# Where the memory-to-memory sums of w_ff2 are issued, and which queue fetches the gates

## The chip, the core and the metric

One of the eight cores of a Trainium2 chip runs the whole kernel. Its engines work side by side, each on a program of its own: TensorE (PE; its weight loads are shown as PEld), VectorE (DVE), ScalarE (ACT), GpSimd (POOL) and SyncE (SP). Sixteen DMA engines move the data; SP and POOL only issue DMAs to them. The metric is the time of one execution in microseconds, lower is better. A run is timed on the chip several times, and one further execution is profiled.

## The reference

One layer of a decoder, 512 tokens by 1024 channels, float32. Cut to what matters:

```python
h = rms_norm(x, norm_mix)
qa, ka, va, u, qm, km, vm, gates = split_in(h @ w_in)
ya = swa_attention(qa, ka, va, sinks) @ w_o_swa              # branch A
z = gelu(s5_ssm(u, ...)) @ w_glu                             # branch B
yb = (z[..., :512] * sigmoid(z[..., 512:])) @ w_o_ssm
yc = moba_attention(qm, km, vm) @ w_o_moba                   # branch C
g = sigmoid(gates)                                           # 3 x 1024 channels
x = x + (g[..., :1024] * ya + g[..., 1024:2048] * yb + g[..., 2048:] * yc) @ w_out
h = rms_norm(x, norm_ffn)
x = x + square(relu(h @ w_ff1)) @ w_ff2                      # 1024 -> 4096 -> 1024
return rms_norm(x, norm_final)
```

## The kernel before

Matrix products run on TensorE in float32r, each as three matmuls: a weight block is split by ScalarE into a high part (`ACT.copy`) and by VectorE into what is left (a subtraction), and high x high, high x low and low x high are accumulated.

**The plan.** All that comes before the output projection is a list, `plan` (lines 223 to 242), of 81 steps, numbered from 0; `do(n, job)` (line 1027) emits one step. "u", "q", "k", "v" and "g" are 128 columns of the input projection (24 matmuls of 512 columns each); "g", b, m is block m of branch b's gates. "oa", "ob", "oc" are 128 columns of the three branch outputs (12 matmuls each), "s", "z" and "y" belong to branch B's GLU, "drain" and "start" steer the attention threads, which are woven between. The steps that matter here:

- 4 to 11: g of branch A; 18, 19, 28 to 35, 38, 39, 60, 69, 73, 76: g of branches B and C
- 20: drain of branch B's state-space part; 40 to 51: oa with y; 52 to 59: s and z
- 61 to 68: ob 0 to 7; 69: g; 70: drain; 71, 72: oc 0, 1; 73: g; 74, 75: oc 2, 3; 76: g; 77 to 80: oc 4 to 7

**Weight blocks.** The class `Stream` (line 158) fetches them on SP's queue, three blocks ahead: when the last part of a block has been split, the load of the third block after it is emitted. A load waits for a free buffer.

**Gates.** A "g" step computes tanh of half the product into `gb` (ScalarE) and, unless it is needed within four steps, stores it to DRAM from POOL's queue (line 1046, `g<-gb`, 23 of the 24). `gate_of` (line 1015) fetches it back into a tile `gl` two steps ahead of the product that it gates (line 1029), from POOL's queue. VectorE then forms (gate + 1) x product from the accumulator, which frees it (lines 1084 and 1087). There are two such accumulators, so TensorE can run one product ahead of VectorE.

**The sums of w_ff2.** The second feed-forward product uses a scheme of the Strassen kind on quarters of 512 x 512 of `w_ff2`, which wants sums of quarters. They are formed in DRAM, in tiles `td[q]`, q = 0 to 6, with four places each, by DMAs alone: a copy of a quarter, or an accumulating DMA that adds one (line 1153) or another place of `td` (lines 1156, 1159). These are POOL's. `w2_sums` (line 1144) is a generator of 56 DMAs of 512 KB, 28 copies and 28 that add; a `next` emits one. From step 14 on, one is emitted after each step (line 1170), so the last belongs to step 69. The first reader of `td` is `load_q` (line 1471), in the second feed-forward product; `load_t` (line 1506) reads the other places later still.

**Order.** The schedule is by hand (`tc.manual_schedule()`): each engine runs its instructions in the order in which they are emitted, and waits at an instruction for what that one needs. SP's and POOL's DMAs are issued in that order too; a DMA that waits holds back all that follow on its queue.

**Behind the plan.** The output projection (lines 1311 to 1334) is four row blocks t of 8 k-steps, 48 matmuls each; its weights `wor` and the residual `x` are fetched on SP's queue from the end of steps 71, 74 and 75 on. Within it the first blocks of `w_ff1` are fetched and split (`parts.ahead`, line 1327). The first feed-forward product runs over `steps`: 16 whole ones (two for each of 8 column blocks), 77 of a Strassen-like scheme over pairs of blocks (7 each), and 4 whole ones. Four of them are written out, the loop at line 1523 runs over the rest, 93.

Of the kernel before, what the change touches and what calls it, by code (L numbers as in the profile page):

```python
# [19 lines left out]
def trunk(ctx: ExitStack, tc: tile.TileContext, x, norm_mix, w_in, sinks, lam_re, lam_im,  # L20
# [50 lines left out]
    class Engine:  # L71
# [42 lines left out]
    PE, ACT, DVE, POOL, SP = (Engine(e, n) for e, n in (  # L114
        (nc.tensor, "PE"), (nc.scalar, "ACT"), (nc.vector, "DVE"), (nc.gpsimd, "POOL"),
        (nc.sync, "SP")))
# [13 lines left out]
    def B8(shape, name, dt=F32):  # L130
        return slot("B8", 18, big.tile(shape, dt, tag="B8", name=nm_(name), bufs=18))

    def B4(shape, name, dt=F32):
        return slot("B4", 11, big.tile(shape, dt, tag="B4", name=nm_(name), bufs=11))

    def B2(shape, name, dt=F32):
        return slot("B2", 7, big.tile(shape, dt, tag="B2", name=nm_(name), bufs=7))
# [4 lines left out]
    def PS(tag, name, shape=(128, 512)):  # L142
        b = {"acc": 2, "S": 3, "T": 2, "O": 1}[tag]
        return slot(tag, b, psum.tile(list(shape), F32, tag=tag, name=nm_(name), bufs=b))
# [13 lines left out]
    class Stream:  # L158
# [7 lines left out]
        def add(self, w, k, cols, width):  # L166
            nk = k // 128
            for c0 in cols:
                if c0 % width == 0 or not self.jobs or self.jobs[-1][1] is not w:
                    self.blocks.append((w, nk, c0, width))  # L170
                for k0 in range(0, nk, 4):
                    self.jobs.append((len(self.blocks) - 1, w, k0, c0))
# [50 lines left out]
    plan = [("u", m) for m in range(4)]  # L223
# [29 lines left out]
    for job in plan:  # L253
        if job[0] in where:
            w, k, c, width = where[job[0]]
# [84 lines left out]
    def stt(o, a, s, b, op0, op1):  # L340
        DVE.scalar_tensor_tensor(o, a, s, b, op0=op0, op1=op1)
# [13 lines left out]
    MUL, ADD, SUB = ALU.mult, ALU.add, ALU.subtract  # L355
# [645 lines left out]
    gd = {(b, m): dram.tile([128, 512], F32, name=f"g{b}_{m}") for b in range(3) for m in range(8)}  # L1001
    gsb, ga, fin, sg = {}, [], {}, {}
# [12 lines left out]
    def gate_of(b, m):  # L1015
        if (b, m) not in gsb:
            gsb[b, m] = B2([128, 512], "gl")
            POOL.dma_start(gsb[b, m], gd[b, m])
        return gsb[b, m]

    def prep_y(m):
# [71 lines left out]
    def more():  # L1093
        if all(x_.over for x_ in build) and not threads["ssm"]:
            threads["ssm"] = [weave(ssm_run(g)) for g in ((0, 2), (1, 3))]
# [38 lines left out]

    NQ, FROM, EACH = 7, 14, 1
    td = [dram.tile([128, 2, 4, 512], F32, name=f"td{q}") for q in range(NQ)]

    def w2_of(q, h, c):  # L1140
        return w_ff2[0][512 * q:512 * q + 512, 512 * c:512 * c + 512].rearrange(
            "(s h p) c -> h p s c", h=2, p=128)[h]

    def w2_sums():
        for r in range(NQ + 3):
            if r < NQ:
                for h, js in ((0, (0, 1)), (1, (2, 3))):
                    for c in range(2):
                        POOL.dma_start(td[r][:, :, js[c]], w2_of(r, h, c))
                        yield  # L1150
            if 0 <= r - 1 < NQ:
                for j, h in ((0, 0), (1, 1)):
                    POOL.dma_start(td[r - 1][:, :, j], w2_of(r - 1, h, 1), accum_op=ADD)
                    yield
            if 0 <= r - 2 < NQ:
                POOL.dma_start(td[r - 2][:, :, 3], td[r - 2][:, :, 0], accum_op=ADD)
                yield
            if 0 <= r - 3 < NQ:
                POOL.dma_start(td[r - 3][:, :, 2], td[r - 3][:, :, 3], accum_op=ADD)
                yield  # L1160

    sums2 = w2_sums()

    ut = B8([128, 4, 4, 128], "ut")
    u_t[0] = ut
    build = [weave(ssm_b()), weave(ssm_c()), weave(ssm_phasors())]
    for n, job in enumerate(plan):
        do(n, job)
        more()
        if n >= FROM:  # L1170
            for _ in range(EACH):
                next(sums2, None)
    for _ in sums2:
        pass

    class Parts:

# [85 lines left out]
    steps, late = [], []  # L1263
# [15 lines left out]
    def tail_part(t, acc, ns):  # L1279
        xs = x2[t // 2][:, t % 2, :]  # L1280
        s_, c_ = st[:, t:t + 1], st[:, 4 + t:5 + t]
        if 0 in ns:
            xn_[t] = B4([128, 1024], "xn")
        for n in ns:
            sl = slice(n * 512, n * 512 + 512)
            stt(xs[:, sl], acc[n], 0.5, xs[:, sl], MUL, ADD)
            ACT.activation(xn_[t][:, sl], xs[:, sl], AF.Square, accum_out=s_)
            if n == 0:
                stt(c_, s_, 1.0 / 1024, eps, MUL, ADD)
# [21 lines left out]
    for t in range(4):  # L1311
        acc = [PS("acc" if t % 2 else "S", "xo") for _ in range(2)]
        for ns in (((0, 1),) if t < 3 else ((0,), (1,))):
            for k in range(8):
                if t == 0 and 2 <= k < 6:
                    prep_w(k + 2)
                a_h = mx_t["h", k // 4][:, k % 4, t * 128:t * 128 + 128]
                a_l = mx_t["l", k // 4][:, k % 4, t * 128:t * 128 + 128]
                b_h, b_l = wo_t["h", k // 2][:, k % 2, :], wo_t["l", k // 2][:, k % 2, :]
                for s_, w_, f in ((a_h, b_h, 0), (a_h, b_l, 1), (a_l, b_h, 2)):  # L1320
                    for n in ns:
                        PE.matmul(acc[n], s_, w_[:, n * 512:n * 512 + 512],
                                  start=(k == 0 and f == 0), stop=(k == 7 and f == 2))
                if k == 5 and t > 0 and 0 in ns:
                    turn(t - 1, prev)
                if 0 in ns and (t, k) in AHEAD:
                    parts.ahead(1)
            tail_part(t, acc, ns)
        if t == 0:
            for _ in range(3):  # L1330
                parts.load()
            h2h = [B8([128, 4, 512], "h2h", F32R) for _ in range(2)]
            h2l = [B8([128, 4, 512], "h2l", F32R) for _ in range(2)]
        prev = tail(t)
# [143 lines left out]
    def b_prep(i, h):  # L1478
        if i < NP:
            t = wb[i, h] = B8([128, 2, 1024], "w2s", F32R)  # L1480
            src = wq[i][:, 2 * h:2 * h + 2].rearrange("p c n -> p (c n)")
            split(t[:, 0], t[:, 1], src)
# [37 lines left out]
            load_t(n + 3)  # L1520

    xs_ = x_sums()
    for u, p in steps[4:]:
        if len(u) == 2:
            for _ in xs_:
                pass
        f1_step(u, p)
        if len(u) == 1:
            next(xs_, None)
        if (u, p) == late[-1]:  # L1530
            load_q(0)
            load_q(1)
            a_sums(0)
            b_prep(0, 0)
        if (u, p) == ((30,), 1):
            a_prep(0)
    while later:
        later.pop()()
    b_prep(0, 1)
    load_q(2)  # L1540
    gf = B4([128, 1024], "gf")
# [22 lines left out]
    for i in range(NP):  # L1564
        q, s_ = divmod(i, 2)
# [30 lines left out]
    for n in range(3 * NQ):  # L1596
        j, q = divmod(n, NQ)
# [72 lines left out]
```

## Time and profile before

| | us |
|---|---|
| median of 3 runs | 825.02 |
| lowest and highest | 822.97, 827.93 |
| the profiled execution | 822.13 |
| its span, from the first to the last instruction | 820.4 |

| engine | busy us | share of the span |
|---|---|---|
| TensorE | 776.0 | 95% |
| VectorE | 590.2 | 72% |
| ScalarE | 439.5 | 54% |
| POOL | 105.1 | 13% |

The profile names an instruction by its engine, its line (L110 is the helper that emits all compute instructions, L90 the one that emits DMAs) and its tiles, out<-in. `x12` is a count; `[1.65 <-DVE gl L110]` says that the engine was idle for 1.65 us before the instruction, and what ended that. PEclk is the granted share of TensorE's full clock. In the table of DMA queues q0 is POOL's queue and q1 SP's. A busy TensorE is not one at its full rate, since matmuls are pipelined and wait within the pipe as well.

### The profile page before, as it was taken

How to read it: one execution, taken by the hardware profiler on the slowest of the kernel's cores; microseconds unless marked ns; L12 is line 12 of the kernel's file. 1: busy time of each engine (PE TensorE's matmuls, PEld its weight loads, DVE VectorE, ACT ScalarE, POOL GpSimd, SP SyncE). 2: the span in 40 equal slices, each digit the busy share in tenths (PEclk: the TensorE clock that was granted, in tenths of full speed). 3: DMA queues.
4: the chain of work that ended last, by engine and by line, in shares of the span. 5: the costliest groups of instructions: out<-in, count | busy, mean ns of one | idle time of the engine just before them, and what ended most of it. 6: DMA issues, size and time to landing. Idle time of an engine off the chain costs nothing.

```text
span 820.4 us, 11497 instructions
## 1 busy us (share of the span) xinstructions
PE 776.0 (95%) x4210; PEld 662.0 (81%) x4210; DVE 590.2 (72%) x1176; ACT 439.5 (54%) x848; POOL 105.1 (13%) x163
## 2 busy tenths in 40 slices
PE   5999999999899999996799999999999999999996
PEld 5887777878788887785678888899999978888885
DVE  6985697774785688773358445788788688976775
ACT  7496633373665566650134434556565565665633
POOL 5131010170021345032210000000000000000000
PEclk9999999999999999999999999999999999999998
DMA  9452371479366999979995004133333476645702
GB/s 248 120 150 74 118 193 56 138 155 249 99 150 183 228 289 246 270 180 207 259 340 185 5 22 127 40 101 103 96 105 102 155 256 205 206 146 187 257 1 103
DMA packets 116249, 130.29 MB, mean 159 GB/s; under 512 B 5304, under 2 KB 87264, under 8 KB 116192
## 3 DMA queue, kind: packets, MB, share of 16 engines
q1 hardware_dynamic: 99232, 85.22, 34.1%
q0 software_dynamic: 16768, 44.06, 22.8%
q8 instruction: 33, 0.54, 0.3%
q10 hardware_dynamic: 192, 0.27, 0.1%
q14 instruction: 24, 0.20, 0.1%
HBM read 119.30 MB, written 37.49 MB: 191 GB/s over the span
## 4 chain that ended last, share of the span: by engine, by line
PE 68%; DVE 14%; DMA 9%; ACT 5%; issue 3%; POOL 1%; DVEq 0%; ACTq 0%; POOLq 0%
PE f L110 36%; PE acc L110 18%; PE xo L110 5%; DVE w L110 4%; DMA wraw<-in_w_in_dram 3%; DMA td<-in_w_ff_dram 2%; DVE own L110 2%; DMA f1raw<-in_w_ff_dram 2%; PE s L110 2%; DVE p L110 2%; PE po L110 2%; PE pt L110 1%; PE y L110 1%; DMA gl<-g 1%; DVE t L110 1%
## 5 line engine op out<-in xcount | busy, mean ns | idle before, releaser
L110 PE MATMUL acc<-hh,w 128*128 128x512 f32 (+1 forms) x672 | 217.7, 390 | 9.7 <-DVE k L110 4.5
L110 PEld LDWEIGHTS acc<-hh,w 128*128 128x128 f32 x672 | 125.8, 191 | 34.9 <-issue 6.8
L110 PE MATMUL acc<-hl,w 128*128 128x512 f32 (+1 forms) x336 | 129.4, 385 | 2.1 <-DVE hl L110 2.1
L110 PE MATMUL f<-h2h,f1w 128*128 128x256 f32 (+1 forms) x456 | 102.9, 313 | 2.8 <-DVE vz L110 2.6
L110 DVE TENSOR_TENSOR w<-wraw,w 128x512 fp32r<-128x512 f32 x112 | 74.8, 686 | 18.6 <-ACT w L110 18.2
L110 ACT CAST w<-wraw 128x512 fp32r<-128x512 f32 x112 | 67.2, 618 | 35.6 <-DMA wraw<-in_w_in_dram 21.9
L110 PEld LDWEIGHTS f<-h2h,f1w 128*128 128x128 f32 x456 | 76.8, 191 | 8.6 <-ACT f1w L110 3.1
L110 PE MATMUL f<-w2s,s 128*128 128x512 f32 x336 | 79.2, 390 | 0.7 <-DVE w2s L110 0.6
L110 PEld LDWEIGHTS f<-w2s,s 128*128 128x128 f32 x336 | 62.9, 188 | 14.6 <-DVE w2s L110 1.0
L110 PEld LDWEIGHTS acc<-hl,w 128*128 128x128 f32 x336 | 64.2, 191 | 12.8 <-DVE hl L110 2.5
L110 PE MATMUL f<-h2l,f1w 128*128 128x256 f32 (+1 forms) x228 | 71.4, 313 | 0.3 <-DVE h2l L110 0.3
L110 PE MATMUL f<-xt,f1w 128*128 128x256 f32 x528 | 67.1, 283 | 0.0
L110 PEld LDWEIGHTS f<-xt,f1w 128*128 128x128 f32 x528 | 65.1, 192 | 0.1
L110 PE MATMUL acc<-o,w 128*128 128x512 f32 x192 | 48.2, 396 | 0.1
L110 ACT ACTIVATE act<-act 128x512 f32<-128x512 f32 (+1 forms) x54 | 31.8, 589 | 27.8 <-DVE act L110 26.8
L110 PEld LDWEIGHTS f<-h2l,f1w 128*128 128x128 f32 x228 | 43.5, 191 | 3.0 <-DVE h2l L110 0.5
L110 ACT CAST w2s<-wq 128x1024 fp32r<-128x1024 f32 x28 | 28.8, 1050 | 27.2 <-PE f L110 12.7
L110 PE MATMUL f<-w2s,av 128*128 128x512 f32 x168 | 42.7, 389 | 0.0
L110 PEld LDWEIGHTS acc<-o,w 128*128 128x128 f32 x192 | 35.1, 188 | 7.9 <-issue 0.9
L110 DVE TENSOR_TENSOR f1w<-f1raw,f1w 128x512 fp32r<-128x512 f32 x53 | 36.0, 685 | 7.4 <-ACT f1w L110 7.4
L90 POOL DMA_DIRECT2D g<-gb x23 | 12.8, 557 | 217.2 <-ACT gb L110 180.6
L110 DVE TENSOR_TENSOR w2s<-wq,w2s 128x1024 fp32r<-128x1024 f32 x28 | 33.5, 1220 | 8.9 <-ACT w2s L110 8.9
(222 smaller groups left out, 1469.1 us busy)
## 6 DMA issues: line engine op xcount, KB each, us to landing
td<-in_w_ff_dram POOLq DMA_DIRECT2D x42, 512.0 KB, 9.9
wraw<-in_w_in_dram SPq DMA_DIRECT2D x40, 512.0 KB, 4.5
f1raw<-in_w_ff_dram SPq DMA_DIRECT2D x32, 512.0 KB, 4.2
tq<-td SPq DMA_DIRECT2D x21, 512.0 KB, 4.5
td<-td POOLq DMA_DIRECT2D x14, 512.0 KB, 12.5
wq<-in_w_ff_dram SPq DMA_DIRECT2D x14, 512.0 KB, 4.4
g<-gb POOLq DMA_DIRECT2D x23, 256.0 KB, 3.5
gl<-g POOLq DMA_DIRECT2D x23, 256.0 KB, 9.9
```

The costliest lines, as they stand in the source:

```text
L90: return f(o, *a, **k)
L110: return f(o, *a, **k)
```

## The change

Three things. Gate loads are issued by SP in place of POOL. The sums are emitted at other places: after steps 13 to 17, after every second step from 26 to 80, once in each of the four row blocks of the output projection, and before every fifth of the 93 steps of the loop over the first feed-forward product; what is left would follow that loop. And their order within the generator is another one: the sums that `load_q` reads first, all seven q, then those of place 1, which is read late. The 56 DMAs are the same.

```diff
     def gate_of(b, m):
         if (b, m) not in gsb:
             gsb[b, m] = B2([128, 512], "gl")
-            POOL.dma_start(gsb[b, m], gd[b, m])
+            SP.dma_start(gsb[b, m], gd[b, m])
         return gsb[b, m]
...
-    NQ, FROM, EACH = 7, 14, 1
+    NQ = 7
+    SUMS_AT = set(range(13, 18)) | set(range(26, len(plan), 2))
...
     def w2_sums():
-        for r in range(NQ + 3):
-            if r < NQ:
-                for h, js in ((0, (0, 1)), (1, (2, 3))):
-                    for c in range(2):
-                        POOL.dma_start(td[r][:, :, js[c]], w2_of(r, h, c))
-                        yield
-            if 0 <= r - 1 < NQ:
-                for j, h in ((0, 0), (1, 1)):
-                    POOL.dma_start(td[r - 1][:, :, j], w2_of(r - 1, h, 1), accum_op=ADD)
-                    yield
-            if 0 <= r - 2 < NQ:
-                POOL.dma_start(td[r - 2][:, :, 3], td[r - 2][:, :, 0], accum_op=ADD)
-                yield
-            if 0 <= r - 3 < NQ:
-                POOL.dma_start(td[r - 3][:, :, 2], td[r - 3][:, :, 3], accum_op=ADD)
-                yield
+
+        def copy(q, j, h, c):
+            POOL.dma_start(td[q][:, :, j], w2_of(q, h, c))
+
+        def add(q, j, src):
+            POOL.dma_start(td[q][:, :, j], src, accum_op=ADD)
+
+        for q in range(NQ + 1):
+            if q < NQ:
+                copy(q, 0, 0, 0)
+                yield
+                copy(q, 3, 1, 1)
+                yield
+                add(q, 0, w2_of(q, 0, 1))
+                yield
+                copy(q, 2, 1, 0)
+                yield
+            if q:
+                add(q - 1, 2, td[q - 1][:, :, 3])
+                yield
+            if q < NQ:
+                add(q, 3, td[q][:, :, 0])
+                yield
+        for q in range(NQ + 1):
+            if q < NQ:
+                copy(q, 1, 0, 1)
+                yield
+            if q:
+                add(q - 1, 1, w2_of(q - 1, 1, 1))
+                yield
...
     for n, job in enumerate(plan):
         do(n, job)
         more()
-        if n >= FROM:
-            for _ in range(EACH):
-                next(sums2, None)
-    for _ in sums2:
-        pass
+        if n in SUMS_AT:
+            next(sums2, None)
...
                 if 0 in ns and (t, k) in AHEAD:
                     parts.ahead(1)
+                if 0 in ns and k == 3:
+                    next(sums2, None)
...
-    for u, p in steps[4:]:
+    for n, (u, p) in enumerate(steps[4:]):
+        if n % 5 == 0:
+            next(sums2, None)
...
     while later:
         later.pop()()
+    for _ in sums2:
+        pass
     b_prep(0, 1)
```

## Rows read from the trace of the kernel before

**Rows 1.** The page: the span, and POOL's DMA queue (packets, MB, share).

```profile
span 820.4 us, 11497 instructions
...
q0 software_dynamic: 16768, 44.06, 22.8%
```

**Rows 2.** Busy time by stage: stretch, length, engines with instructions, PEclk, DMA share, GB/s.

```profile
361.00:438.00 77.00, 65.88 (x269) 51.68 (x267) 39.57 (x61) 19.98 (x34) 18.68 (x26) 0.96 0.99 265
438.00:485.00 47.00, 46.71 (x218) 38.50 (x217) 25.17 (x40) 18.74 (x36) 0.00 (x0) 1.00 0.14 37
485.00:640.00 155.00, 151.86 (x1130) 145.27 (x1129) 118.37 (x203) 91.91 (x176) 0.00 (x0) 1.00 0.34 94
```

**Rows 3.** Waits, 361 to 438 us: total, times, longest.

```profile
PE acc L110 <- DVE gl L110: 11.0, 5, 4.4
...
DVE gl L110 <- DMA gl<-g: 27.3, 7, 7.0
```

**Rows 4.** Timeline of TensorE, 361 to 440 us: start, length, instruction, idle before.

```profile
388.26 4.58 PE L110 MATMUL acc<-z,w 128*128 128x512 f32 x12 [2.88 <-DVE gl L110]
...
408.53 0.50 PE L110 MATMUL acc<-hh,w 128*128 128x512 f32 x1 [4.40 <-DVE gl L110]
...
427.12 11.04 PE L110 MATMUL acc<-o,w 128*128 128x512 f32 x48
```

**Rows 5.** Timeline of POOL, 363 to 405 us.

```profile
365.64 1.52 POOL L90 DMA_DIRECT2D gl<-g  x1
...
396.89 0.88 POOL L90 DMA_DIRECT2D td<-td  x1 [8.93 <-DMA td<-td]
397.45 0.91 POOL L90 DMA_DIRECT2D gl<-g  x1
```

**Rows 6.** Timeline of SP, then of POOL, 320 to 352 us.

```profile
326.42 19.21 SPq L90 DMA_DIRECT2D wraw<-in_w_o_ssm_dram  x4
...
348.86 0.57 POOL L90 DMA_DIRECT2D gl<-g  x1 [19.10 <-PE po L110]
```

**Rows 7.** TensorE's waits, 140 to 146 us, then 200 to 212 us.

```profile
PE acc L110 <- DVE k L110: 1.9, 1, 1.9
...
PE acc L110 <- DVE k L110: 2.5, 1, 2.5
```

**Rows 8.** Timeline of POOL: three of the gate stores.

```profile
288.69 0.55 POOL L90 DMA_DIRECT2D g<-gb  x1 [5.80 <-ACT gb L110]
...
363.36 0.56 POOL L90 DMA_DIRECT2D g<-gb  x1 [11.62 <-ACT gb L110]
...
419.06 0.55 POOL L90 DMA_DIRECT2D g<-gb  x1 [12.19 <-ACT gb L110]
```

**Rows 9.** DMA, 380 to 400 us: queues; issues with size and median landing.

```profile
q0 software_dynamic: 1552, 3.37, 83.9%
q1 hardware_dynamic: 1770, 1.15, 23.7%
...
wraw<-in_w_in_dram SPq DMA_DIRECT2D x1, 512.0 KB, 19.2
```

**Rows 10.** DMA, 405 to 440 us, then 485 to 640 us.

```profile
f1raw<-in_w_ff_dram SPq DMA_DIRECT2D x4, 512.0 KB, 9.5
...
q1 hardware_dynamic: 28180, 14.36, 33.2%
```

**Rows 11.** Timeline of SP from 420 us, then of ScalarE from 455 us.

```profile
428.13 68.00 SPq L90 DMA_DIRECT2D f1raw<-in_w_ff_dram  x7
...
458.64 0.63 ACT L110 CAST f1w<-f1raw 128x512 fp32r<-128x512 f32 x1
...
463.94 1.13 ACT L110 CAST f1w<-f1raw 128x512 fp32r<-128x512 f32 x2
```

## The prediction

> **What bounds the kernel now.** I read the page first, then busy time by stage, then TensorE's waits, then the DMA queues. The page gives a span of 820.4 us [rows 1]; the whole profiled execution took 822.13 us. TensorE works nearly all the time, so a gain can only come from a stretch in which it starves. By stage, 361 to 438 us (the gate products "ob" and "oc" of branches B and C, and the last three gate projections) has 65.88 us of TensorE work in 77.00 us, at a mean granted clock of 0.96, with the DMA engines 0.99 busy; the output projection behind it has 46.71 of 47.00 us and DMA at 0.14; the first feed-forward product has 151.86 of 155.00 us and DMA at 0.34 [rows 2]. So one stage starves, it is the one whose DMA engines are full, and the two stages behind it have DMA time to spare.
>
> What starves it: TensorE waits five times, 11.0 us, for VectorE's step that reads a gate tile and frees the accumulator, and VectorE waits 27.3 us, seven times, for gate loads [rows 3]. Why the gate loads are late: they stand in POOL's queue between the sums. A load issued at 365.64 us is behind the sums of the steps before it. The sum at 396.89 us first had POOL sit 8.93 us for another sum to land, and the gate load right behind it, at 397.45 us, is the one for which TensorE stood still until 408.53 us [rows 4, 5]. The chip adds a second charge: after the longer idle times the granted clock was at the lower of its two levels, 1.2 instead of 2.4 GHz. Twelve matmuls from 388.26 us took 4.58 us, against 11.04 us for 48, or 2.76 us for 12, later in the stage [rows 4].
>
> **The change, part by part.**
>
> Gate loads. 23 loads leave POOL's queue for SyncE's; no load is added, each step has the loads it had. On POOL they no longer stand behind a wait for a landed sum. The bound of the gain is the 11.0 us of waits plus the clock: 0.04 of 77 us is 3.1 us [rows 2, 3]; 14.1 us together. I do not take all of it. Five sums still go out behind the gate store of 363.36 us (steps 60 to 68), where ten stood before, and the gate loads still need DMA time beside them; one stall of the smaller kind (11.0 / 5 = 2.2 us) may be left. I take 12.5 us, ends 8 and 14.1.
>
> What is queued behind them on SyncE: the weight blocks, `w_out` and `x`. On POOL a gate load's wait for a free buffer (released by the attention product) lasted 19.10 us once, but POOL was early there: what counts is how late the buffer comes free against the weight load behind it. That wait ended at 348.86 us; SyncE's fourth `w_o_ssm` load had gone out by 345.63 us, so at worst 3.2 us of hold [rows 6]. The buffers of the later gate loads are released by the gate products four to five steps before, so nothing waits long. I cost this at nothing, since weight blocks are fetched three blocks ahead; if that cover were gone it would be about 3.2 us, once.
>
> Sums taken out of the early part. In place of one sum a step from step 14 on, there are five at steps 13 to 17 and one every second step from 26. So behind the branch-B drain one sum follows where eight did. There a weight block landed late and the wait of TensorE for the K projection was 2.5 us, against 1.9 us for the same step of branch A with idle DMA engines [rows 7]. The gain is 0.6 us, and at most another 1.7 us if the clock no longer drops afterwards; I take 1 us, ends 0 and 2.3.
>
> Where the sums go. This is the part to be careful with. The text says "every fifth feed-forward step", but a DMA on POOL waits for nothing that TensorE does: it is held only by what stands ahead of it in POOL's program and by the sum whose result it needs. What paced POOL were the gate stores, which wait for ScalarE, as at 288.69, 363.36 and 419.06 us [rows 8]; the one at 419.06 us (step 73) is the last store. In the changed kernel POOL has only sums after it. Counting the generator: 5 in steps 13 to 17, 28 in steps 26 to 80, 4 in the output projection, 19 in the feed-forward steps, 56 as before; 29 of them are issued up to step 72, and 27 stand behind the last store. These 27 will run as one train, starting near 419 - 13 = 406 us, not spread to 640 us.
>
> Its length: POOL's queue moved 44.06 MB in 22.8% of 820.4 us, 4.25 us a MB, so a sum of 0.524 MB takes 2.2 us of all 16 engines [rows 1]. 27 of them are 60 us at the least. Some of that time goes to SyncE's loads and some to waiting for a landed sum (an accumulate waits for the copy it adds to); I expect the train to end between 480 and 500 us. Before, nothing of POOL's moved in that time.
>
> What the train meets: two `w_out` loads, `x`, the last gate loads, then the first `w_ff1` blocks. With sums in flight the queues take turns packet by packet: from 380 to 400 us 1552 packets of POOL's and 1770 of SyncE's went through, taking 83.9% and 23.7% of the engines, 0.173 and 0.043 us a packet [rows 9]. A `w_ff1` block is fetched in packets of 14.36 MB / 28180 = 510 bytes, 1028 of them [rows 10]: alone 1028 x 0.043 / 16 = 2.8 us of the queue, with a sum's packet before each one 1028 x 0.216 / 16 = 13.9 us. So the first three blocks land about 11, 22 and 33 us later than they do now. Now they are issued from 428.13 us on, land 9.5 us later (median), and ScalarE casts the first at 458.64 us and needs the second within the pair at 463.94 us [rows 10, 11]: 21 us of cover for the first, about 24 us for the second. The first is just covered. The second, and the third behind it, may come some us late, and with ScalarE standing the residual sums behind it stand as well. I price this at 3 us, plus 2 us for the second pair of `w_out` loads and the last gate loads, which now follow `x` in SyncE's queue: 5 us, ends 0 and 18 (the second end is the rival's below).
>
> The Trainium skill, "DMA: Bandwidth & Descriptors", section "Queues, rings and completion order", says that each DMA engine goes round its queue rows one packet at a time. The packet counts above agree with it, 1552 against 1770 [rows 9]. By that rule the gate loads lose something by the move: on POOL's row they had a turn of their own beside the weights, on SyncE's they share one turn with the weights. It speaks for the second rival below, whose time is worked out there from rows.
>
> The sum: 12.5 + 1 - 5 = 8.5 us off the profiled execution's 822.13 us, 813.6 us. The median of the runs before is 825.02 us, 2.9 us above the profiled one, so 816.5 us stands beside it.
>
> **The rivals.**
>
> First: the train is harmless. For it speaks that the output projection now leaves the engines 0.86 idle and that the first `w_ff1` block has 21 us of cover [rows 2, 11]. Then 14.1 + 1.5 us are gained, 809.5 us.
>
> Second, on the other side: the train and SyncE's order starve the end of the stage. The gate loads of the last "oc" steps stand behind two `w_out` loads and four `x` loads in one queue. 4 MB in 4 KB packets are 1024 packets; with a sum's packet each, 1024 x 0.173 / 16 = 11.1 us are added. Behind them the third and the fourth `w_out` load (another 5.5 us) and the `w_ff1` blocks wait, whose second one then comes 22 + 16 - 24 = 14 us after it is needed. If the 11.1 us fall on TensorE in full, and half of the 14 us, the cost is 18 us: 13.5 - 18 = 4.5 us slower, 829.5 us. It decides from the point where the gate load of "oc" 5 lands later than two gate products (5.5 us) after its turn. Against it: now, too, these loads share the engines with gate loads and a sum from 405 to 440 us, and TensorE doesn't wait after 409 us.
>
> Third: the gate loads are as late on SyncE as on POOL, behind weight blocks, of which one took 19.2 us from issue to landing among the sums [rows 9]. Then the 11 us stay and only the clock and the early part change; with the train's 5 us it is no change, 825 us. Against it: only five sums, not ten, meet this stage.
>
> **How the numbers follow.** A measurement of this kernel can tell about 0.5%, 4.1 us, from no change. Forecast (4 to 13 us gained) 0.44; harmless train 0.18; no change 0.17; slower 0.21. Faster holds the first two, 0.62. The likeliest time is 816.5 us, its own range 812 to 821. The range of all cases: below, the full bounds with a harmless train, 825.02 - 14.1 - 2.3 = 808.6, less the 2 us by which the fastest run before lies under the median, 806.6; above, the slower rival, 829.5 us, cut to 829 so that under 2 in 10 is left out.
>
> **What the profile of the changed kernel would show.** TensorE's waits for the gate step gone or under 3 us from 361 to 425 us, granted clock back at 0.98 or more there; POOL's queue busy without a gap from about 406 to 490 us and empty after it, not one sum every fifth step to 640 us; `w_ff1` blocks landing in 12 us or more up to 490 us, and ScalarE waiting for one or two of them. I am wrong if the gate step is still waited for, if sums really come one by one up to 640 us, or if TensorE stands for more than 8 us between 425 and 500 us.

## The result and the profile after

The changed kernel takes 804.27 us (median of four runs, 800.91 to 807.01) against 825.67 us (822.97 to 827.93) of the kernel before: ratio 0.974, 95% interval 0.9692 to 0.9789. The forecast was 816.5 us and the range 806.6 to 829.0. The direction was right, the size was not: 21 us came instead of 8.5, and the time lies below the range. The profiled execution took 800.91 us, 21.2 us less than the one of before.

The page of the changed kernel: the span, POOL's busy tenths in 40 slices, SyncE's queue (q1), POOL's queue (q0), and the group of POOL's sums with their idle time.

```profile
span 799.1 us, 11512 instructions
...
POOL 6041020040011231001212131000000000000000
...
q1 hardware_dynamic: 102544, 91.26, 37.1%
q0 software_dynamic: 14928, 38.03, 20.8%
...
L90 POOL DMA_DIRECT2D td<-in_w_ff_dram x42 | 36.3, 1078 | 76.2 <-DMA td<-in_w_ff_dram 75.5
```

Busy time by stage, columns as in [rows 2]; the last row is the stretch that holds the same TensorE work as the first of [rows 2].

```profile
361.00:438.00 77.00, 77.00 (x345) 63.88 (x344) 49.57 (x72) 26.88 (x42) 14.43 (x18) 1.00 1.04 307
438.00:485.00 47.00, 46.14 (x258) 39.71 (x257) 22.89 (x39) 17.92 (x38) 12.05 (x14) 1.00 0.89 192
485.00:640.00 155.00, 151.56 (x1101) 143.81 (x1100) 120.47 (x206) 94.95 (x176) 2.09 (x2) 1.00 0.46 127
356.00:416.50 60.50, 60.50 (x269) 50.10 (x268) 39.55 (x61) 20.20 (x34) 11.98 (x15) 1.00 1.03 320
```

The waits of the changed kernel, 361 to 438 us, the longest three and VectorE's for the gate tile's product.

```profile
POOL td L90 <- DMA td<-in_w_ff_dram: 31.5, 3, 11.0
POOL g L90 <- ACT gb L110: 19.3, 2, 10.9
ACT mh L110 <- DVE ga L110: 17.5, 8, 3.1
DVE gl L110 <- PE acc L110: 15.8, 10, 4.9
```

POOL's timeline around its last gate store and at its end.

```profile
395.83 0.59 POOL L90 DMA_DIRECT2D g<-gb  x1 [8.40 <-ACT gb L110]
396.41 1.44 POOL L90 DMA_DIRECT2D td<-in_w_ff_dram  x2
407.83 1.77 POOL L90 DMA_DIRECT2D td<-in_w_ff_dram  x2 [9.99 <-DMA td<-in_w_ff_dram]
408.97 1.61 POOL L90 DMA_DIRECT2D td<-td  x1
418.35 0.90 POOL L90 DMA_DIRECT2D td<-td  x1 [7.77 <-issue]
...
493.95 1.05 POOL L90 DMA_DIRECT2D td<-in_w_ff_dram  x1 [5.45 <-DMA td<-in_w_ff_dram]
```

The stage that starved [rows 2, 3] starves no more. VectorE now waits for TensorE's product where it waited for the gate load, TensorE waits for neither, and the granted clock is 1.00. TensorE's 269 matmuls of that stretch take 60.50 us; before they took 77.00 us, 65.88 of them busy. So 16.5 us came from there: 11.1 us of idle time and 65.88 - 60.50 = 5.4 us by which the matmuls themselves took longer before. The lower clock is only a part of these: a mean of 0.96 over 77 us lacks 0.04 x 77 = 3.1 us (3.5 at most, by the rounding), and the clock can't have cost more than that. Another part is the new start after each wait. Before, two groups of twelve matmuls ran behind waits of 1.2 and 1.7 us at a granted clock of 1.00 and took 3.00 us each, against 2.76 us for twelve in an unbroken run [rows 4]. Five such starts are about 1.2 us; some 1 us stays unexplained. The first of the two groups, and the mean clock around it:

```profile
374.35 3.00 PE L110 MATMUL acc<-z,w 128*128 128x512 f32 x12 [1.65 <-DVE gl L110]
...
360.00:380.00 20.00, 17.18 (x75) 13.58 (x75) 10.48 (x17) 6.18 (x12) 10.11 (x13) 1.00 0.86 160
```

The rest is read from the starts of the same matmul in both traces: 1.0 us lost in the first 60 us, 1.6 won between 165 and 175 us, 3.6 won between 187 and 260 us, 0.8 won up to 361 us, 16.5 won up to 438 us, and from there to the end nothing above 0.8 us either way. The train of sums ran from 396.41 to 493.95 us and then nothing; it cost TensorE no more than these 0.8 us. The sums that read `w_ff2` itself stood 76.2 us in all before they went out, 75.5 of them for a copy that had to land; a group like that is not among the large ones of the kernel before.

One effect of the change stands neither in its text nor in the prediction. The kernel weaves the attention threads into the plan by a model of time of its own (`account`, `step`), which counts every DMA that is emitted. With one sum behind the drain of branch B in place of eight, 219 of TensorE's 4210 matmuls stand in another order, between 197 and 257 us. The kernels below with eight sums there have the order of before, the others that of the changed kernel. It matters little: with the new order of the sums, the kernels with eight sums there win 4.1 to 4.2 us between 187 and 260 us, the changed kernel 3.6.

### The profile page after: what moved, and what is told of

It is laid out like the page before. It is cut to its first block, busy times and chain, and to the rows that moved or that the text cites. A ratio compares the mean times of both kernels' runs of the same rounds, so it can differ in the third digit from the quotient of the medians.

```text
span 799.1 us, 11512 instructions
## 1 busy us (share of the span) xinstructions
PE 768.6 (96%) x4210; PEld 658.5 (82%) x4210; DVE 589.3 (74%) x1176; ACT 440.0 (55%) x848; POOL 92.2 (12%) x140
## 4 chain that ended last, share of the span: by engine, by line
PE 77%; DVE 13%; DMA 4%; ACT 3%; issue 2%; DVEq 0%; ACTq 0%
PE f L110 37%; PE acc L110 26%; PE xo L110 5%; DVE w L110 4%; DVE own L110 2%; DMA f1raw<-in_w_ff_dram 2%; PE s L110 2%; PE po L110 2%; PE pt L110 2%; DMA wraw<-in_w_in_dram 2%; PE y L110 1%; DVE t L110 1%; PE pg L110 1%; DVE pr L110 1%; DVE p L110 1%
## 5 line engine op out<-in xcount | busy, mean ns | idle before, releaser
L110 PE MATMUL acc<-hh,w 128*128 128x512 f32 (+1 forms) x672 | 215.3, 386 | 3.2 <-DVE k L110 1.9
L90 POOL DMA_DIRECT2D td<-in_w_ff_dram x42 | 36.3, 1078 | 76.2 <-DMA td<-in_w_ff_dram 75.5
```

The source lines that it names most:

```text
L90: return f(o, *a, **k)
L110: return f(o, *a, **k)
```

## The experiments

A sum below is one of the 56 memory-to-memory copies or accumulates of `w_ff2`. The change has three parts: the queue of the gate loads (POOL or SyncE), the places of the sums (one a step, or thinned out and a train), and the order of the sums among themselves. The prediction priced the first two. The ratio stands for each kernel against the runs of before on the same chip. The last three columns are what the profiled execution wins (or loses, with a minus) against the profiled one of before in three stretches of before's time, read from the starts of the same matmuls.

| order of the sums | gate loads on | places | us | ratio, 95% interval | 300 to 335 | 361 to 438 | 438 to 485 |
|---|---|---|---|---|---|---|---|
| old | POOL | old (before) | 825.67 | 1 | | | |
| old | SyncE | old | 827.37 | 0.9998 (0.9956 to 1.004) | -7.2 | 5.3 | 0.0 |
| old | SyncE | new | 823.71 | 0.9996 (0.9962 to 1.0031) | -3.1 | 15.9 | -17.3 |
| new | POOL | old | 815.91 | 0.9914 (0.9882 to 0.9946) | -3.0 | 6.4 | 0.1 |
| new | SyncE | old | 809.97 | 0.9804 (0.9746 to 0.9863) | 0.0 | 7.2 | 0.0 |
| new | POOL | new | 809.10 | 0.9786 (0.9745 to 0.9828) | 0.0 | 10.2 | -0.3 |
| new | SyncE | new (after) | 804.27 | 0.974 (0.9692 to 0.9789) | 0.0 | 16.5 | 0.0 |

The eighth combination (old order, POOL, new places) was not run. The stretches show what the ratios hide. In the starved stage (361 to 438 us) queue and places do nearly all, 15.9 of 16.5 us with the old order; queue and order with a sum a step win 7.2 us. What the new order adds to queue and places lies elsewhere: 17.3 us in the output projection and 3.1 us near 320 us are no longer lost.

### The queue alone, and the sums alone

Gate loads on SyncE, nothing else:

```
-            POOL.dma_start(gsb[b, m], gd[b, m])
+            SP.dma_start(gsb[b, m], gd[b, m])
```

> The gate loads alone go from POOL's queue to SyncE's; the sums stay one a step from step 14 on. Theory (two separate gains, both needed: gate loads off POOL, and fewer sums beside the two stages; and a train of sums behind the last gate store that costs nothing): the waits of TensorE for the gate step from 361 to 438 us shrink from 11.0 us but don't vanish, because ten sums, not five, still take turns with the loads there; the K projection's wait at 204 us stays at 2.5 us. 815 to 820 us. Rival A (the move of the gate loads is all that counts): gate waits zero, clock 1.00 in that stage, 16.5 us gained, 806 to 810 us. Rival B (the gate loads are late on either queue while ten sums run beside them; only the new places of the sums count): 823 to 826 us.

Measured: 827.37 us, ratio 0.9998. The theory's 815 to 820 us were missed; rival B's 823 to 826 us are the nearest. The move that my forecast, together with thinner sums, put at 12.5 us brings nothing by itself. Its TensorE waits, 300 to 345 us and then 361 to 438 us:

```profile
PE acc L110 <- DVE ga L110: 3.5, 1, 3.5
...
PE acc L110 <- DVE gl L110: 7.1, 3, 6.8
```

From 361 to 438 us the same matmuls lose 5.3 us less than before, so something is won there; but 7.2 us are lost between 300 and 335 us, 3.5 of them in a wait that before did not have. DMA issues from 303 to 309 us, with the median landing:

```profile
gl<-g SPq DMA_DIRECT2D x2, 256.0 KB, 15.4
td<-in_w_ff_dram POOLq DMA_DIRECT2D x1, 512.0 KB, 24.9
```

A gate load is off POOL's queue and still takes 15.4 us. No wait of POOL's is in front of it any more, but weight blocks share its queue, and in these 6 us 379 packets of POOL's queue went beside 367 of SyncE's.

The changed kernel with the gate loads back on POOL (the same line, the other way):

> The sums stand where the change puts them; the gate loads stay on POOL's queue. Theory (two separate gains): the early gain of about 5 us up to 236 us is there in full; from 361 to 438 us gate loads still stand behind accumulates that wait for a landed copy, now every second step, so 5 to 10 us of the 16.5 us come: 806 to 814 us. Rival A (the move of the gate loads is all that counts in the stage): gate waits stay near 11 us, 818 to 821 us. Rival B (only the sums count): gate waits gone, 802 to 806 us.

Measured: 809.1 us, 0.9786, as the theory had it. Of the stage's 16.5 us, 10.2 came without the move of the gate loads. Rival A, that only the move counts, is out. So is rival B, that only the sums count: TensorE still waits 3.3 us for gate products, and 5 us more come with the move. I had still not seen the third part.

### The order of the sums

The changed kernel's order with the old places (one sum a step from step 14), gate loads on SyncE:

```
-    SUMS_AT = set(range(13, 18)) | set(range(26, len(plan), 2))
+    SUMS_AT = set(range(14, len(plan)))
```

> The gate loads on SyncE's queue, and the changed kernel's order of the sums (which copy comes before which accumulate), but one sum a step from step 14 on, as before. Only the order differs from the first experiment, which was 827.4 us. Theory (with no gate load on POOL nothing but gate stores and landed sums holds the sums back, eight of them are in flight at once, and the gate tiles on SyncE's queue take 15 us and more): the new waits near 320 us and near 395 us come back, together over 8 us: 815 to 828 us. Rival (the order's own waits are what thins the sums): no such wait, 801 to 810 us.

Measured: 809.97 us, 17 us below the first experiment, which differs in the order alone; my theory missed it and the rival was right in time. In the trace it was right near 320 us, where the wait is gone. In the stage TensorE still waits for gate products (361 to 438 us):

```profile
PE acc L110 <- DVE gl L110: 7.0, 3, 5.3
```

The timeline of POOL from 292 to 330 us, first the kernel with the old order, a few rows:

```profile
310.78 0.91 POOL L90 DMA_DIRECT2D td<-td  x1 [3.42 <-DMA td<-td]
316.36 0.89 POOL L90 DMA_DIRECT2D td<-td  x1 [4.68 <-DMA td<-td]
318.07 0.72 POOL L90 DMA_DIRECT2D td<-in_w_ff_dram  x1 [0.82 <-DMA td<-in_w_ff_dram]
321.55 0.69 POOL L90 DMA_DIRECT2D td<-in_w_ff_dram  x1 [2.76 <-DMA td<-in_w_ff_dram]
```

and then the one with the new order:

```profile
294.69 1.77 POOL L90 DMA_DIRECT2D td<-in_w_ff_dram  x2
305.23 1.78 POOL L90 DMA_DIRECT2D td<-in_w_ff_dram  x2 [8.78 <-DMA td<-in_w_ff_dram]
306.38 1.60 POOL L90 DMA_DIRECT2D td<-td  x1
314.25 0.89 POOL L90 DMA_DIRECT2D td<-td  x1 [6.28 <-DMA td<-in_w_ff_dram]
```

Both wait for landed sums, but not for the same ones. In the old order an accumulate of this stretch stands nine or more sums behind the one that it needs. By the numbers POOL stops only when about eight are in flight (24.9 us to landing, with one issued every 2.9 us from 293 to 325 us: 24.9 / 2.9 = 8.6). One goes out whenever one lands, so the queue should hardly ever be empty. In the new order an accumulate stands two to five sums behind the one that it needs, so POOL issues three and then stops 6 to 11 us until one of these has landed.

The other two corners. The new order alone, all else as before:

> The kernel before with the changed kernel's order among the sums and nothing else: gate loads on POOL's queue, one sum a step. Theory (the new order's waits hold the sums, but on POOL's queue the gate loads stand behind just these waits): the K projection's wait at 204 us goes (4 us), the gate waits from 361 to 438 us stay or grow, 815 to 824 us. Rival (the order is the whole gain): 803 to 810 us.

Measured: 815.91 us, 0.9914, within the theory's numbers. The wait at 204 us is gone. TensorE's waits for gate products shrank from 11.0 to 6.8 us, where the theory had them stay or grow. That what is left comes from gate loads standing behind the new waits fits, but no run isolates it.

The changed kernel with the old order:

```
-            if q < NQ:
-                copy(q, 0, 0, 0)
-                yield
...
+            if r < NQ:
+                for h, js in ((0, (0, 1)), (1, (2, 3))):
+                    for c in range(2):
+                        POOL.dma_start(td[r][:, :, js[c]], w2_of(r, h, c))
+                        yield
...
```

> The changed kernel (gate loads on SyncE's queue, the sums at the changed places) with the order of before among the sums: four copies of a block of rows first, their accumulates one to three rounds later. Theory (the new order is a third part of the change, with a gain of its own: an accumulate soon behind its copy makes POOL wait for a landed sum, so that few sums are in flight, while in the old order eight are in flight and SyncE's loads take 20 us and more): gate tiles and weight blocks land later again, TensorE waits for them, and the train packs closer: 808 to 818 us. Rival (the places and the queue suffice, the order only mattered with a sum in each step): 800 to 806 us, without gate waits.

Measured: 823.71 us, 0.9996: without the order the other two parts together bring nothing, which is beyond both expectations. The stage is cured here too; TensorE's wait for gate products, 361 to 438 us:

```profile
PE acc L110 <- DVE gl L110: 0.3, 1, 0.3
```

But 3.1 us are lost near 320 us, and the train takes the rest back in the output projection. The waits from 438 to 485 us of this kernel's own time:

```profile
ACT f1w L110 <- DMA f1raw<-in_w_ff_dram: 27.8, 3, 12.2
...
PE h L110 <- DVE xn L110: 10.9, 1, 10.9
```

The matmuls that ran from 438 to 485 us before run from 420 to 485 us here and lose 17.3 us. This is one half of my second rival: ScalarE stands at a `w_ff1` cast, and the residual sums stand behind it. The other half, 11.1 of its 18 us, was to come from late gate loads, and those are not late (0.3 us); it had about 7 us for the `w_ff1` blocks. That 18 and 17.3 lie so close is luck.

The DMA queues and the `w_ff1` loads from 430 to 480 us, in this kernel:

```profile
q0 software_dynamic: 3555, 8.45, 86.3%
q1 hardware_dynamic: 3579, 1.96, 19.5%
...
f1raw<-in_w_ff_dram SPq DMA_DIRECT2D x3, 512.0 KB, 49.8
```

in the changed kernel:

```profile
q0 software_dynamic: 2800, 6.91, 69.0%
q1 hardware_dynamic: 5325, 2.68, 21.0%
...
f1raw<-in_w_ff_dram SPq DMA_DIRECT2D x5, 512.0 KB, 12.9
```

Where POOL's queue always holds a sum, each packet of SyncE's has one of POOL's before it, 3555 to 3579. A packet of POOL's is 0.863 x 50 x 16 / 3555 = 0.194 us, one of SyncE's 0.044 us, so a block of 1028 packets takes 1028 x 0.238 / 16 = 15.3 us; three in the queue are 46 us, and they took 49.8. Where POOL's queue runs empty, SyncE sends nearly two packets for one.

Do fewer sums run in the changed kernel, then? Not over the whole train. POOL's queue in the changed kernel, 396 to 494 us, then in the one with the old order, 399 to 495 us:

```profile
q0 software_dynamic: 5617, 14.15, 64.9%
...
q0 software_dynamic: 5826, 13.32, 71.0%
```

The bytes are nearly the same; how they are spread is not. By the DMA packets of the traces, from 430 to 480 us the kernel with the old order has no moment without a packet of POOL's, the changed kernel 5.6 us.

The Trainium skill, "DMA: Bandwidth & Descriptors", section "Queues, rings and completion order", says that an engine goes round the queue rows for which it has work. The prediction took the first half of that sentence; these rows agree with the second half too: with a row that is empty for a part of the time, its neighbour sent 5325 packets to 2800, not 3579 to 3555.

### By what the order acts

To the changed kernel with the old order, I added a copy of 512 bytes after every third sum, from a sum's result to a scratch tensor, so that POOL has to wait as in the new order. First it reads the first of the three, then the third:

```
+            done.append((q, jj))
+            if len(done) % 3 == 0:
+                q_, j_ = done[-3]          # then: done[-1]
+                POOL.dma_start(brk[...], td[q_][0:1, 0, j_, 0:128])
```

(The text calls the changed kernel with the old order the eighth experiment.)

> The kernel of the eighth experiment (changed queue, changed places, order of before among the sums; 823.7 us), and in addition POOL copies 512 bytes of the first of every three sums to a scratch tensor, so that it has to wait for that sum to land before it goes on. The added copies are work that the reference doesn't need. Theory (the order matters through these waits alone: they empty POOL's queue from time to time, and SyncE's loads then go without a sum's packet before each of theirs): sums land in 7 to 14 us, the w_ff1 blocks in 15 to 27 us instead of 41 to 56 us, TensorE no longer stands 17 us at 438 to 485 us: 801 to 809 us. Rival (something else in the order, such as which rows are copied next to which): 815 to 825 us.

Measured: 816.39 us, 0.991: within the rival's range, above the theory's. Two sums are still in flight at each wait, POOL's packets hold 77.4% of the engines' time from 430 to 480 us, and `w_ff1` blocks take 27.1 us. The output projection loses 3.0 us in place of 17.3, but 7.6 us are lost behind it, up to 560 us. So this run does not decide.

> As the last experiment, but the added copy of 512 bytes reads the third of every three sums, not the first, so that POOL waits until its queue is empty (it is work that the reference doesn't need). With the first of three, two sums were still in flight at each wait, and half of the difference came: 816.4 us between 823.7 (old order) and 804.3 us (new order). Theory (what counts is how often POOL's queue runs empty): the w_ff1 blocks land in 10 to 27 us, no stand of TensorE at 415 to 540 us beyond 3 us, 802 to 809 us. Rival (the waits give half at most, the rest is something else in the order): 812 to 818 us again.

Measured: 811.53 us, 0.9845 (0.9768 to 0.9922), four runs from 808.56 to 818.59: between the two ranges, half a microsecond below the rival's. The time decides nothing, but the trace of the profiled execution (810.16 us) is the theory's up to 515 us. The same view of the queues, 430 to 480 us:

```profile
q0 software_dynamic: 2425, 6.38, 56.1%
q1 hardware_dynamic: 5554, 2.80, 20.3%
...
f1raw<-in_w_ff_dram SPq DMA_DIRECT2D x5, 512.0 KB, 8.5
```

From 187 to 515 us every matmul starts 3.0 us after the same one of the changed kernel: nothing is won or lost there. (Nearly all of the 3.0 us are two falls of the clock, near 146 and 173 us.) What it has more, 6.6 us between 515 and 549 us, goes with the train's length: with these waits its last sum goes out at 532 us, not at 494 us, and TensorE waits 7.7 us for VectorE's `vz` from 485 to 640 us, the wait of the longer trains below. So in this execution the waits by which POOL's queue runs empty account for all that the order does up to there; the order's own waits do it in less time.

### How long a train is free

The changed kernel with no sum in the steps of the plan, all 56 in the train; and with 16 ahead and 40 in the train:

```
-    SUMS_AT = set(range(13, 18)) | set(range(26, len(plan), 2))
+    SUMS_AT = set(range(13, 18)) | set(range(26, 48, 2))     # 40; for 56: none in the plan
...
+    for _ in range(17):                                      # 27 for 56
+        next(sums2, None)
```

> The changed kernel, but no sum runs in the planned steps: all 56 stand behind the last gate store in POOL's queue, so the train is twice as long. Theory (the train of 27 was free only because the loads of the w_ff1 blocks have about 20 us of cover, and one landed 0.02 us ahead of its use): a train of 56 sums runs from about 400 to beyond 590 us, each w_ff1 block takes near 14 us instead of 9.5 us while two are needed every 10.4 us, the cover runs out, TensorE waits in the first feed-forward product: 820 to 850 us. Rival (sums beside that product cost nothing at any length): 800 to 805 us, with the loads late by no more than in the changed kernel.

Measured: 849.02 us, ratio 1.026.

> The changed kernel with 40 sums behind the last gate store instead of 27: the ones of plan steps 48 to 80 are taken out of the plan and stand right behind it. Theory (the loads of the w_ff1 blocks have a cover that the train of 27 just uses up: one landed 0.02 us ahead of its use; 56 in the train cost 45 us): the train ends near 545 us, blocks issued from 500 to 540 us take 12 to 15 us instead of 4 to 9, TensorE waits in the first feed-forward product for 10 to 25 us: 812 to 828 us. Rival (the train of 27 is far from its limit; that of 56 costs so much because it reaches some later stage): 800 to 806 us.

Measured: 819.09 us, 0.9899. Both as the theory had it. The longest wait of TensorE from 485 to 640 us, first with 56 sums in the train, then with 40:

```profile
PE f L110 <- DVE vz L110: 38.2, 6, 11.0
```

```profile
PE f L110 <- DVE vz L110: 14.5, 5, 10.2
```

A train of 27 is nearly free, 13 more cost 15 us, 16 further ones 30 us. The limit is near 27: in the changed kernel ScalarE waits once for a `w_ff1` block, at the train's end.

```profile
487.12 0.62 ACT L110 CAST f1w<-f1raw 128x512 fp32r<-128x512 f32 x1 [2.79 <-DMA f1raw<-in_w_ff_dram]
```

### The early part

The changed kernel with eight sums behind the drain of branch B again, where the prediction saw the gain of its second term, and seven fewer in the train:

```
-    SUMS_AT = set(range(13, 18)) | set(range(26, len(plan), 2))
+    SUMS_AT = set(range(13, 18)) | set(range(20, 28)) | set(range(28, len(plan), 2))
```

> The changed kernel, with one sum behind each of steps 20 to 27 again (eight behind the drain of branch B, where the change leaves one or two); so seven sums fewer are in the later train. Theory (the eight sums made the K projection's weight block land late, and the 3.4 us lost at 204 us, K wait and the lower clock after it, come from that): the wait of 2.5 us and the lower clock return at 200 to 210 us, 3.5 to 5.5 us slower than the changed kernel, 808 to 810 us. Rival (the K wait is not of the sums, and the early gain is another chance of the clock): no wait at 204 us, 803 to 805 us.

Measured: 801.64 us, 0.9706 (0.9672 to 0.9739), below the rival's range too. The theory fell: with the new order the eight sums bring no wait of the K projection back. Beside the changed kernel on one chip:

> The changed kernel once more, to stand beside the next run on the same chip: 801 to 806 us. If the fall of the clock at 170 us is chance, it may or may not be there; all else as in the first execution.

> The changed kernel with eight sums behind the drain of branch B (the third experiment again), beside the changed kernel on the same chip. Theory (in the new order seven more sums at 177 to 206 us cost nothing there, and seven fewer in the train take away the small waits at 540 to 580 us, 0.7 us): within 2 us of the changed kernel, more likely below it. Rival (they bring the K projection's wait back in some executions): 3 us above it.

Measured: 802.77 us (802.25 to 803.92) and 800.94 us (799.48 to 801.99). Beside each other this version is some 2 us below the changed kernel, six runs each without an overlap. That is less than it looks: of the 2.6 us between the two profiled executions, 1.6 are the clock at 170 us, which fell in the changed kernel's and not in the other's (below), and over all runs of the two kernels the ranges overlap (800.91 to 807.01 us and 799.09 to 805.03 us in the first ones). The two profiled executions in which the clock stayed up, 800.91 and 799.64 us, differ by 1.3 us. That this version is faster is likely, and not shown.

The kernel before once more:

> The kernel before, unchanged, one more execution with a profile. The profiled execution of before had the lower clock for part of 170 to 187 us, and then a K projection's wait of 2.5 us with the lower clock again at 204 us; every variant so far, with or without sums there, lacks the second. Theory (the first fall of the clock is chance; the late weight block at 204 us follows from it, because the block is then issued behind six queued sums instead of three): either both are there again, or, if the clock stays up at 170 us, the block lands by 197 us and TensorE waits for nothing at 204 us. Rival (the wait of 2.5 us belongs to before's order of loads and sums): it is there whatever the clock does at 170 us.

Measured: the clock stayed up at 170 us and the wait at 204 us came all the same, 3.5 us. So the wait does not follow from the fall of the clock; the rival was right. The granted clock from 170 to 187 us, before again and then the changed kernel again:

```profile
170.00:187.00 17.00, 17.00 (x83) 14.27 (x84) 13.50 (x50) 11.63 (x37) 13.33 (x21) 1.00 0.88 191
```

```profile
170.00:187.00 17.00, 16.62 (x74) 14.02 (x75) 13.59 (x54) 11.71 (x38) 8.20 (x15) 0.90 0.63 155
```

In the first executions it was the other way round, 0.90 before and 1.00 after. TensorE waits 1.9 us for VectorE ahead of this stretch in all of them; whether the clock falls behind it differs from execution to execution, and is worth 1.6 us. The K projection's wait came with the old order only: with a sum a step it was 2.5, 3.5, 0.7 and 0 us in four executions (before twice, the next experiment, the first one); with the new order and as many sums there it was absent in all four, and with one sum there or none in all eight, the old order among them. So in these sixteen executions it came with the old order and many sums only, and even then not always; what decides is open.

Last, the old order with branch A's gate loads on POOL and the others on SyncE:

```
-            POOL.dma_start(gsb[b, m], gd[b, m])
+            (POOL if b == 0 else SP).dma_start(gsb[b, m], gd[b, m])
```

> The kernel before, with the gate loads of branch A left on POOL's queue and those of branches B and C on SyncE's; the sums one a step, as before. Theory (in the first experiment a gate load on POOL, which waits there for its buffer, was missing as a brake on the sums up to 330 us, and that alone made a gate tile land 15.6 us after its issue and TensorE wait 7 us near 320 us): that wait is gone, while 361 to 438 us is as in the first experiment (5 us less than before, or more): 810 to 819 us. Rival (sums in that number delay the gate tiles on whichever queue they stand): a wait of several us near 320 us stays, 820 to 828 us.

Measured: 817.83 us, 0.989 (0.982 to 0.9961). The time is the theory's, the trace is not: between 300 and 335 us half of the loss is still there (3.7 us, a wait of 2.1 us for a product's step), and in the stage TensorE waits 10.7 us for gate products. That a gate load on POOL brakes the sums stays a guess.

## Why the prediction was wrong

**What bounds the kernel** was read rightly: the stage of 361 to 438 us starved for gate tiles [rows 2, 3], and 16.5 of 21.2 us came from it.

**The step that failed is the train's term, minus 5 us, and with it a term that is missing.** The change has a third part, the order of the sums, and I gave it no term. I named the fact that would have priced it, that an accumulate waits for the copy it adds to, only for the train's length, as a delay. The changed kernel with the old order is the change as I priced it. There the stage wins 15.9 us and the stretch from 187 to 260 us 3.6, where I had 12.5 and 1; the train costs 17.3 us, where I had 5; 3.1 us are lost near 320 us, where I had nothing; and all of it together is a gain of 0.04%, with an interval that holds zero. The new order takes the two losses away: nothing is lost near 320 us, and at most 0.8 us behind 438 us. Alone it is worth 0.9%.

**Gate loads off POOL, 12.5 us.** I priced the move together with the five sums that were to meet the stage in place of ten, and so it was right in kind: 15.9 us in the old order, 16.5 in the new. The move alone is another thing: with ten sums beside them the gate waits shrink from 11.0 to 7.1 us only, 7.2 us are lost near 320 us, and the time stays (0.02%, interval 0.9956 to 1.004). My third rival, "as late on SyncE as on POOL", is half right for that kernel, and the ground on which I set it aside, five sums and not ten, was a good one: with the old order and five sums the gate waits are 0.3 us. The bound was too low, 14.1 us for 16.5. The idle time (11.1 us) and the clock (3.1 us) in it were right; what I left out is that the matmuls start anew after every wait.

**Fewer sums behind the drain, 1 us.** 3.6 us came between 187 and 260 us, the wait [rows 7] and the lower clock behind it. The cause is open: eight sums stand there at no cost in the new order, and in the old one the wait came in three executions of four. Another 1.6 us at 170 us is chance of the clock.

**The train, minus 5 us.** Its place, start and end were nearly right: 27 sums from 396 us, the last out at 494 us. The price of a block among sums (13.9 us) was right for a queue that is never empty, 15.3 us by the rows of the changed kernel with the old order. What such a queue costs was not: 17.3 us, and 5 was my price. But I wrote that the queue would be busy without a gap, and in the changed kernel it is not: POOL's packets hold 69.0% of the engines' time from 430 to 480 us, against 86.3% with the old order. (That POOL stands, 55.9 of the 104 us from 396 to 500 us behind copies that have to land, does not tell this by itself: with the old order it stands 75.8 us there, and its queue is never empty from 430 to 480 us.) I also had only two things that hold a sum back, POOL's program and the sum that it needs; about eight sums in flight are a third. The blocks of 430 to 480 us land 12.9 us after their issue and nothing stands. A longer train costs what I feared.

**Of what the profile was to show**, the gate waits and the clock came as said, POOL empty after 490 us too, `w_ff1` blocks in 12 us or more too; ScalarE's wait for one or two of them was one of 2.8 us, which TensorE does not see.

## What to carry to other kernels

What low-priority copies on a queue of their own cost is set by two things: how many of them run beside the loads that matter (thinned out, they let the starved stage go in either order), and how often their queue runs empty (the same train costs 17.3 us when it never does). Let each few of them wait for a landed one (an accumulate put soon behind its copy does this for nothing), and check afterwards that what has to land still lands in time. When a diff rewrites a generator, compare the order of what it yields before pricing where it is called. And read the gain of each variant by stretch: two parts that bring nothing together can hide 15.9 us won and 17.3 us lost.

## What was unexpected of the hardware

- With POOL's queue never empty, SyncE's loads of small packets got one packet for each of POOL's: 3579 for 3555, and a block of 512 KB in 510-byte packets took 49.8 us (median of three). With gaps in POOL's queue such blocks took 12.9 us (median of five), and POOL still moved 6.91 MB in those 50 us instead of 8.45.
- With about eight sums in flight, one took 24.9 us from issue to landing; of three that were issued together in the same stretch (303 to 309 us) two took 9.8 us (median) and one 15.3.
- Where TensorE waits 11.1 us in pieces of 1 to 4.4 us, its matmuls take another 5.4 us more, of which the lower clock is 3.1 (mean granted clock 0.96). Twelve matmuls behind a wait took 3.00 us at a granted clock of 1.00, against 2.76 in an unbroken run.
- After one and the same wait of 1.9 us the granted clock from 170 to 187 us was 0.90 or 1.00, from execution to execution of one kernel.
